# Shift and scale worked out in four quarters of the channels, with the first three weight slabs taken quarter by quarter, in a one-core transformer layer

## The chip, the cores and the metric

One core of one Trainium2 chip runs the whole program. The metric is the device time of one execution in microseconds. Three runs of the kernel before took 1442.45, 1448.24 and 1449.41 us, so the median is 1448.24 us. One more execution was profiled, and all rows below come from it.

## The reference, cut to what matters

```python
def modulation(cv, w, b):
    m = jax.nn.silu(cv) @ w + b                      # w is 1024 x 6144
    return [a[:, None, :] for a in jnp.split(m, N_MOD, axis=-1)]
...
m_lat = modulation(c, w_mod[l], b_mod[l])
m_ctx = modulation(c_ctx[None], w_mod[l], b_mod[l])
u_lat = rmsnorm(x, g[0]) * (1.0 + m_lat[1]) + m_lat[0]
u_ctx = rmsnorm(ctx, g[0]) * (1.0 + m_ctx[1]) + m_ctx[0]
y_lat, y_ctx = token_mixer(u_lat, u_ctx, ...)         # starts with u @ w_in, 1024 x 8704
x = x + m_lat[2] * rmsnorm(y_lat, g[1])
f_lat = moe(...)                                      # 32 experts, 1024 x 2048 and 1024 x 1024 each
x = x + m_lat[5] * rmsnorm(f_lat, g[3])
```

There are 256 latent and 256 context tokens of 1024 channels, in float32. Only the first two of the six modulation vectors, shift and scale, matter to the change. They are needed before the first product with w_in.

## The kernel before, in words

**Set-up (lines 104 to 148).** Two rows of c and c_ctx go through a sigmoid and are transposed to `csT`, which is 128 channels by 8 groups of channels by 32 columns (two of them used). The tokens x and ctx are loaded into `xt` and `xn[:, 2:4]` by two transfers of 1 MB, which SP issues (lines 120 and 121).

**Shift and scale (`mod_first`, line 168, and `mod_columns`, line 154).** For each half `hv` of the channels, 4 MB of w_mod are loaded in eight transfers of 512 KB into the tiles tagged `oh` and `oa`. 32 matmuls, each with 32 columns of the array and 256 moving columns, gather the sums in the PSUM tile `pm`. ScalarE copies `pm` out to `mr`, TensorE transposes it to `pmt`, and VectorE adds the bias into `mod`.

**Inputs (lines 278 to 287).** ScalarE squares each of four token tiles and takes a root, VectorE scales the tile, TensorE transposes it in blocks into `xT`, and ScalarE copies these to `xnT`, which has one column block for each of eight groups of 128 channels.

**Modulated inputs (`modulated`, line 293).** For each channel group `k`, two ScalarE activations of 256 tokens apply scale and shift in `xnT`. VectorE rounds the result to `uh` (fp32r) and puts the rest in `ul`.

**Slabs.** A slab is 1024 rows by 256 columns of w_in, which is 1 MB in runs of 1 KB (`slab`, line 225). A ScalarE cast gives its upper part `hi`, a VectorE subtraction the rest `lo`; `hl` holds both, in two buffers. Each product is three matmuls (`mm3`, line 246). The first three slabs, two of the forget gates (`pf`, 512 moving columns) and one of the values (`pv`, 256 moving columns), are worked through in two halves of the channels (lines 315 to 329). The third slab is loaded over `xn`, and so its transfer waits for the last transpose of the inputs.

**What sets the order.** A scheduler orders each engine's instructions when the program is built; each engine then runs its list in that order, and SP issues its transfers in its order too. After the slabs above come more slabs and the recurrence (up to some 300 us), attention, merge and router (to some 515 us), and the experts. The experts' weights come through a ring of ten 2 MB buffers (`Ring`, line 897), which is refilled as TensorE finishes with a buffer.

Of the kernel before, what the change touches and what calls it, by code (L numbers as in the profile page):

```python
# [11 lines left out]
F32 = mybir.dt.float32  # L12
F32R = mybir.dt.float32r
# [9 lines left out]
P = 128  # L23
D = 1024
KT = 8
# [14 lines left out]
def hybrid_layer(ctx, tc, x, c, ctx_in, c_ctx, w_mod, b_mod, norm_g, w_in, hgrn_lb, hgrn_norm_g,  # L40
                 qk_norm_g, w_branch, w_out, router_w, router_b, w_up, b_up, w_down, b_down,
                 rope_c, rope_s, out):
    nc = tc.nc
    pe, act, dve, pool = nc.tensor, nc.scalar, nc.vector, nc.gpsimd
# [46 lines left out]
    def mmps(name):  # L91
        return ps.tile([P, 512], F32, tag="mm", bufs=4, name=name)
# [24 lines left out]
    nc.scalar.dma_start(small_l, hgrn_lb.rearrange("d l (k p) -> (d l k) p", p=P))  # L117
    xn = xp.tile([P, 4, D], F32, tag="xn", name="xn")
    xnT = xp.tile([P, KT, 512], F32, name="xnT")
    nc.sync.dma_start(xt, x.rearrange("b (t p) d -> p (b t) d", p=P))  # L120
    nc.sync.dma_start(xn[:, 2:4], ctx_in.rearrange("b (t p) d -> p (b t) d", p=P))

# [44 lines left out]

    def mod_first(hv):

        pm = trps(f"pm0{hv}")  # L170
        wv = w_mod[0, :, 0:2048].rearrange("(q k p) (i f) -> p q k i f", k=2, p=P, i=2)
        for q in range(4):
            if q % 2 == 0:
                wq = lp.tile([P, 2, 2, 2, 512], F32, tag=("oh", "oa")[q // 2], name=f"wm0{hv}{q}")
            wr = wq[:, q % 2]
            for k in range(2):
                nc.sync.dma_start(wr[:, k], wv[:, q, k, :, hv * 512:(hv + 1) * 512])
                for j in range(4):
                    pe.matmul(pm[32 * j:32 * j + 32, 0:256], csT[:, 2 * q + k],
                              wr[:, k, j // 2, (j % 2) * 256:(j % 2) * 256 + 256],  # L180
                              start=q + k == 0, stop=q + k == 4)
        mod_columns(pm, 256, 2, (8, 2), 4 * hv, f"0{hv}")

    def mod_steps(ch, acc):

# [51 lines left out]

    def split(hi, lo, src):

        act.copy(hi, src)  # L240
        dve.tensor_sub(lo, src, hi)  # L241
# [4 lines left out]
    def mm3(o, a, b, k, opens, closes):  # L246

        i = pe.matmul(o, a[0], b[0], start=k == 0 and opens, stop=False)  # L248
        if k == 0 and not opens:
            tc.keep_in_program_order(i)  # L250
        pe.matmul(o, a[0], b[1], start=False, stop=False)  # L251
        pe.matmul(o, a[1], b[0], start=False, stop=k == KT - 1 and closes)  # L252

    def chan_major(sl, mh, ml, n, outs, hfs=(0, 1)):

        for hf in hfs:
            hi, lo = sl(hf)
            for cc in range(2):
                for kk in range(4):
                    k = hf * 4 + kk  # L260
                    wh, wl = hi[:, kk, cc * P:(cc + 1) * P], lo[:, kk, cc * P:(cc + 1) * P]
                    mm3(outs[cc], (wh, wl), (mh[hf][:, kk, 0:n], ml[hf][:, kk, 0:n]), k,
                        cc == 0 or n == 512, cc == 1 or n == 512)

    def tok_major(sl, mh, ml, tts, outs, hfs=(0, 1), closes=False):

        for hf in hfs:
            hi, lo = sl(hf)
            for i, tt in enumerate(tts):
                for kk in range(4):  # L270
                    k = hf * 4 + kk
                    th, tl = mh[hf][:, kk, tt * P:(tt + 1) * P], ml[hf][:, kk, tt * P:(tt + 1) * P]
                    mm3(outs[i], (th, tl), (hi[:, kk], lo[:, kk]), k, i % 2 == 0, i % 2 == 1 or closes)
# [16 lines left out]
    uh, ul = [[t[:, hv] for hv in range(2)] for t in uhl]  # L290
    wi = w_in[0]

    def modulated(hv):
        ks_ = slice(4 * hv, 4 * hv + 4)
        for r in range(2):
            dve.scalar_tensor_tensor(aff0[:, r, ks_], mod[:, r, 8 + 4 * hv:12 + 4 * hv], 1.0, gT[:, ks_],
                                     op0=ALU.add, op1=ALU.mult)
        for k in range(4 * hv, 4 * hv + 4):
            for r in range(2):
                sl = xnT[:, k, r * 256:(r + 1) * 256]  # L300
                act.activation(sl, sl, AF.Identity, bias=mod[:, r, k:k + 1], scale=aff0[:, r, k:k + 1])
            dve.tensor_copy(uh[hv][:, k % 4], xnT[:, k])
            dve.tensor_sub(ul[hv][:, k % 4], xnT[:, k], uh[hv][:, k % 4])

    def part(sl, hf):

        hl = sl(hf)
        return lambda h: hl if h == hf else sl(h)

    def both(sl):  # L310

        hl = [sl(hf) for hf in range(2)]
        return lambda h: hl[h]

    mod_first(0)
    firsts = [(part(slab(wi[:, 2048 + 1024 * d:2304 + 1024 * d], f"f{d}0"), 0),
               [mmps(f"pf0{d}{cc}") for cc in range(2)]) for d in range(2)]
    modulated(0)
    sl_i = slab(wi[:, 1024:1280], "i0", xp.tile([P, 4, D], F32, tag="xn", name="wi0").rearrange("p a b -> p (a b)")[:, 0:2048])
    mod_first(1)  # L320
    for sl, pf in firsts:
        chan_major(sl, uh, ul, 512, pf, (0,))
    pv0 = [hgps(f"pv0{i}") for i in range(2)]
    pvs0 = [pv0[i // 2][:, (i % 2) * 256:(i % 2) * 256 + 256] for i in range(4)]
    tok_major(sl_i, uh, ul, range(4), pvs0, (0,))
    modulated(1)
    for sl, pf in firsts:
        chan_major(sl, uh, ul, 512, pf, (1,))
    tok_major(sl_i, uh, ul, range(4), pvs0, (1,))

    nc.sync.dma_start(hg, hgrn_norm_g.rearrange("l p -> p l"))
    nc.sync.dma_start(rw.rearrange("p (j i) e -> p j i e", i=2), router_w.rearrange("l (j p i) e -> p (l j) i e", p=P, i=2))
# [910 lines left out]
```

## Time and profile before

| | us |
|---|---|
| median of 3 runs | 1448.24 |
| lowest, highest run | 1442.45, 1449.41 |
| profiled execution, its own time | 1452.08 |
| its span | 1450.2 |
| TensorE matmuls busy | 1339.9 (92%) |
| VectorE busy | 504.5 (35%) |
| ScalarE busy | 354.5 (24%) |
| DMA read from HBM | 479.15 MB, 331 GB/s over the span |

The profiled execution lies 3.84 us above the median, and its time is 1.9 us longer than its span. Busy shares are means over stages with different limits, so they say little about one stage. TensorE can run at one of two clock levels, 1.2 and 2.4 GHz, and the profile gives the granted clock of a stretch as a share of the upper one. A timeline row gives start, duration, engine, line, operation, tiles, shape and count, and in brackets how long the engine stood idle before and what ended that.

### The profile page before, as it was taken

The page shows a single profiled execution, that of the slowest core. Times are in us where ns is not written, and L with a number is a line of the kernel's source. Part 1 is how long each engine was busy: PE and PEld are TensorE (multiplying, and loading weights), DVE is VectorE, ACT ScalarE, POOL GpSimd, SP SyncE. Part 2 cuts the span into 40 slices and gives each one's busy share as a digit, 9 for nine tenths or more (in the row PEclk, how much of TensorE's full clock was granted, in tenths as well). Part 3 has the DMA queues.
Part 4 walks back from the last instruction along what each step waited for, and adds up shares of the span by engine and source line. Part 5 has one row for each costly group of instructions (what it writes and reads, how often), then busy time and mean ns, then how long its engine had stood idle before and what let it go on. Part 6 is the DMA issues. An engine that isn't in the chain of part 4 may idle for free. (4 is left out here: it accounts for less than half of the span.)

```text
span 1450.2 us, 18975 instructions
## 1 busy us (share of the span) xinstructions
PE 1339.9 (92%) x8151; PEld 743.0 (51%) x8151; DVE 504.5 (35%) x917; ACT 354.5 (24%) x648; POOL 3.8 (0%) x16
## 2 busy tenths in 40 slices
PE   6999999998999989999998897998899889889887
PEld 3789788898889943333432342342243233224222
DVE  4697777678875341111101011120011010111012
ACT  5444444456555330110100010010010010001002
POOL 0000000000000000000000000000000000000000
PEclk9999999999999899999999999999999999999999
DMA  9535342246649499999999999999999999999994
GB/s 343 173 120 168 121 147 90 88 128 228 225 153 344 150 388 428 428 427 428 426 428 428 428 427 425 427 428 428 427 428 428 427 426 427 428 428 427 428 425 161
DMA packets 88529, 481.52 MB, mean 332 GB/s; under 512 B 5604, under 2 KB 56264, under 8 KB 62072
## 3 DMA queue, kind: packets, MB, share of 16 engines
q1 hardware_dynamic: 87536, 479.24, 81.5%
q8 instruction: 66, 1.08, 0.3%
q10 hardware_dynamic: 776, 0.84, 0.2%
q14 instruction: 23, 0.19, 0.0%
q0 software_dynamic: 128, 0.16, 0.0%
HBM read 479.15 MB, written 1.08 MB: 331 GB/s over the span
## 5 line engine op out<-in xcount | busy, mean ns | idle before, releaser
L847 PE MATMUL pu<-w,xe 128*64 128x512 f32 x2048 | 457.9, 597 | 61.1 <-DMA w<-in_w_up_dram 61.1
L847 PEld LDWEIGHTS pu<-w,xe 128*64 128x64 f32 x2048 | 142.6, 137 | 360.0 <-issue 249.6
L991 DVE TENSOR_SCALAR gl<-pu 128x512 f32<-128x512 f32 (+1 forms) x33 | 22.2, 675 | 617.8 <-PE pu L847 602.5
L847 PE MATMUL py<-w,aT 128*64 128x512 f32 (+1 forms) x1040 | 227.3, 589 | 1.9 <-ACT aT L1033 1.9
L847 PEld LDWEIGHTS py<-w,aT 128*64 128x64 f32 x1040 | 70.9, 137 | 153.5 <-issue 119.3
L992 ACT ACTIVATE sg<-gl 128x512 f32<-128x512 f32 (+1 forms) x33 | 20.2, 616 | 514.9 <-PE pat L850 479.8
L1046 ACT COPY ysb<-py 128x512 f32<-128x512 f32 x31 | 18.1, 585 | 242.2 <-PE py L847 242.2
L847 PE MATMUL acc<-ysb,cw 64*128 64x512 f32 (+2 forms) x260 | 65.8, 608 | 2.7 <-DVE ysb L1189 1.9
L847 PE MATMUL pgx<-oh,xt 128*128 128x256 f32 x256 | 60.2, 394 | 0.0
L847 PEld LDWEIGHTS pgx<-oh,xt 128*128 128x128 f32 x256 | 46.7, 199 | 16.8 <-issue 5.7
L248 PE MATMUL pf<-uh,hlf 128*128 128x512 f32 x128 | 52.3, 414 | 3.1 <-ACT hlf L240 3.1
L252 PE MATMUL pf<-uh,hlf 128*128 128x512 f32 x128 | 52.9, 415 | 0.0
L251 PE MATMUL pf<-ul,hlf 128*128 128x512 f32 x128 | 52.4, 411 | 0.0
L975 DVE TENSOR_SCALAR xe<-pgx,aff,mod 128x256 f32<-128x256 f32 x32 | 17.4, 543 | 88.9 <-PE pgx L847 88.9
L983 DVE TENSOR_SCALAR ow<-iota,posb,comb 128x128 f32<-128x128 f32 x64 | 19.2, 343 | 57.4 <-PE pcw L850 29.5
L248 PE MATMUL pga<-uh,hlga 128*128 128x256 f32 x128 | 36.9, 288 | 2.4 <-ACT hlga L240 2.4
L252 PE MATMUL pga<-uh,hlga 128*128 128x256 f32 x128 | 36.3, 284 | 1.0 <-DVE hlga L241 1.0
L248 PE MATMUL pv<-hli,uh 128*128 128x256 f32 x128 | 36.5, 285 | 0.0
L847 PEld LDWEIGHTS acc<-ysb,cw 64*128 64x128 f32 (+1 forms) x260 | 23.4, 186 | 25.6 <-issue 21.9
L251 PE MATMUL pv<-hli,uh 128*128 128x256 f32 x128 | 36.3, 284 | 0.0
L251 PE MATMUL pga<-ul,hlga 128*128 128x256 f32 x128 | 36.2, 283 | 0.0
L252 PE MATMUL pv<-hli,ul 128*128 128x256 f32 x128 | 36.2, 283 | 0.0
(382 smaller groups left out, 2069.8 us busy)
## 6 DMA issues: line engine op xcount, KB each, us to landing
w<-in_w_up_dram SPq DMA_DIRECT2D x128, 2048.0 KB, 39.1
w<-in_w_down_dram SPq DMA_DIRECT2D x62, 2048.0 KB, 39.1
wm<-in_w_mod_dram SPq DMA_DIRECT2D x16, 1024.0 KB, 4.8
wm<-in_w_mod_dram SPq DMA_DIRECT2D x16, 512.0 KB, 10.3
wf<-in_w_in_dram SPq DMA_DIRECT2D x8, 1024.0 KB, 5.2
wga<-in_w_in_dram SPq DMA_DIRECT2D x8, 1024.0 KB, 5.1
wwb<-in_w_branch_dram SPq DMA_DIRECT2D x8, 1024.0 KB, 6.3
wi<-in_w_in_dram SPq DMA_DIRECT2D x4, 1024.0 KB
```

The costliest lines, as they stand in the source:

```text
L248: i = pe.matmul(o, a[0], b[0], start=k == 0 and opens, stop=False)
L251: pe.matmul(o, a[0], b[1], start=False, stop=False)
L252: pe.matmul(o, a[1], b[0], start=False, stop=k == KT - 1 and closes)
L847: tc.keep_in_program_order(pe.matmul(*args, **kw))
L975: dve.tensor_scalar(xe[:, k], pg, aff2[:, k:k + 1], mod[:, 0, 24 + k:25 + k], op0=ALU.mult, op1=ALU.add)
L983: dve.tensor_scalar(ow[:, tt], view(iota, [[0, 2], [1, CAP]]), posb[:, tt, e:e + 1], comb[:, tt, e:e + 1], op0=ALU.is_equal, op1=ALU.mult)
L991: dve.tensor_scalar(gl, glu_ps, 7.0, None, op0=ALU.min)
L992: act.activation(sg, gl, AF.Sigmoid, scale=1.702)
L1046: act.copy(ysb, py)
```

## The change

Each of the two halves of shift and scale becomes two quarters of 256 channels. A quarter's weights are two transfers of 1 MB in runs of 1 KB (runs of 2 KB before), one for shift and one for scale, into a whole `oh` or `oa` tile (`mod_load`). The first quarter is issued ahead of x and ctx. `mod_first` works with 128 moving columns instead of 256, so it has 32 matmuls for a quarter where it had 32 for a half. The first three slabs are loaded in halves (`send`), and are split and multiplied in quarters of the channels, one after the other for all three slabs. What is computed stays the same.

```diff
+    wmq = [lp.tile([P, 2, KT, 256], F32, tag=t, name="wm0" + t) for t in ("oh", "oa")]
+
+    def mod_load(q):
+
+        wv = w_mod[0, :, 0:2048].rearrange("(k p) (i f) -> p k i f", p=P, i=2)
+        for i in range(2):
+            nc.sync.dma_start(wmq[q % 2][:, i], wv[:, i, :, q * 256:(q + 1) * 256])
+
+    mod_load(0)
     nc.sync.dma_start(xt, x.rearrange("b (t p) d -> p (b t) d", p=P))
     nc.sync.dma_start(xn[:, 2:4], ctx_in.rearrange("b (t p) d -> p (b t) d", p=P))
...
-    def mod_first(hv):
-
-        pm = trps(f"pm0{hv}")
-        wv = w_mod[0, :, 0:2048].rearrange("(q k p) (i f) -> p q k i f", k=2, p=P, i=2)
-        for q in range(4):
...
-                nc.sync.dma_start(wr[:, k], wv[:, q, k, :, hv * 512:(hv + 1) * 512])
-                for j in range(4):
-                    pe.matmul(pm[32 * j:32 * j + 32, 0:256], csT[:, 2 * q + k],
...
-        mod_columns(pm, 256, 2, (8, 2), 4 * hv, f"0{hv}")
+    def mod_first(q):
+
+        pm, wq = trps(f"pm0{q}"), wmq[q % 2]
+        for k in range(KT):
+            for j in range(4):
+                pe.matmul(pm[32 * j:32 * j + 32, 0:P], csT[:, k], wq[:, j // 2, k, j % 2 * P:(j % 2 + 1) * P],
+                          start=k == 0, stop=k == KT - 1)
+        mod_columns(pm, P, 2, (8, 1), 2 * q, f"0{q}")
...
-    def modulated(hv):
-        ks_ = slice(4 * hv, 4 * hv + 4)
+    def modulated(q):
+        hv, ks_ = q // 2, slice(2 * q, 2 * q + 2)
...
-    mod_first(0)
-    firsts = [(part(slab(wi[:, 2048 + 1024 * d:2304 + 1024 * d], f"f{d}0"), 0),
...
+    send(0, 0)
+    send(1, 0)
+    mod_load(1)
+    send(2, 0)
+    for q in range(4):
+        mod_first(q)
+        modulated(q)
+        if q < 2:
+            mod_load(q + 2)
+        if q == 0:
+            for n in range(3):
+                send(n, 1)
+        hv = q // 2
+        for n in range(3):
+            hl = ip.tile([P, 2, 2, 256], F32R, tag="hl", bufs=2, name=f"hl0{q}{n}")
+            hi, lo = hl[:, 0], hl[:, 1]
+            split(hi, lo, wr0[n][:, 2 * q:2 * q + 2])
+            for cc in range(2 if n < 2 else 4):
+                for kk in range(2):
...
```

SP's list, from its third transfer on, before and then in the changed kernel (`wm` is w_mod, `wf` and `wi` the slabs, `xt` and `xn` the inputs):

```order
L120 DMA xt<-in_x_dram 128x2x1024
L121 DMA xn<-in_ctx_dram 128x2x1024
L177 DMA wm_214<-in_w_mod_dram 128x2x512 x4
L177 DMA wm_235<-in_w_mod_dram 128x2x512 x4
L228 DMA wf_263<-in_w_in_dram 128x8x256
L228 DMA wf_270<-in_w_in_dram 128x8x256
L228 DMA wi_295<-in_w_in_dram 128x8x256
L177 DMA wm_298<-in_w_mod_dram 128x2x512 x4
```

```order
L126 DMA wm0oh<-in_w_mod_dram 128x8x256 x2
L129 DMA xt<-in_x_dram 128x2x1024
L130 DMA xn<-in_ctx_dram 128x2x1024
L318 DMA wf_217<-in_w_in_dram 128x4x256
L318 DMA wf_218<-in_w_in_dram 128x4x256
L126 DMA wm0oa<-in_w_mod_dram 128x8x256 x2
L126 DMA wm0oh<-in_w_mod_dram 128x8x256
L318 DMA wi_219<-in_w_in_dram 128x4x256
L126 DMA wm0oh<-in_w_mod_dram 128x8x256
L318 DMA wf_217<-in_w_in_dram 128x4x256
L318 DMA wf_218<-in_w_in_dram 128x4x256
L318 DMA wi_219<-in_w_in_dram 128x4x256
```

Two transfers of w_mod now stand ahead of the inputs, and the transfer of the third slab, which is laid over `xn`, stands ahead of half of the third quarter of w_mod and of the slabs' second halves.

ScalarE's list at the inputs, before and then in the changed kernel (`mr` is the copy of the sums for shift and scale):

```order
L280 ACTIVATE xnT,ssq<-xt 128x1024 x2
L221 ACT_TABLE_LOAD
L221 ACTIVATE rs_146<-ssq,epsc 128x1 x2
L280 ACTIVATE xnT,ssq<-xn 128x1024 x2
L221 ACTIVATE rs_146<-ssq,epsc 128x1 x2
```

```order
L167 COPY mr_264<-pm_231 128x128
L282 ACTIVATE xnT,ssq<-xt 128x1024 x2
L223 ACT_TABLE_LOAD
L223 ACTIVATE rs_150<-ssq,epsc 128x1 x2
L282 ACTIVATE xnT,ssq<-xn 128x1024 x2
L223 ACTIVATE rs_150<-ssq,epsc 128x1 x2
L242 CAST hl_285<-wf_217 128x512
```

The copy of the first quarter's sums now stands ahead of the squares of x.

TensorE's list at the border of the third and the fourth quarter in the changed kernel, and VectorE's list at the same place (`hl_605` and `hl_620` are the fourth quarter's weights; `bf` and `bu` belong to the experts' bias):

```order
L254 MATMUL pv_225<-hl_529,ul 128x256
L171 MATMUL pmt_591<-ident,mr_589 128x128
L250 MATMUL pf_220<-uh,hl_605 128x512
L250 MATMUL pf_221<-uh,hl_605 128x512
L250 MATMUL pf_222<-uh,hl_620 128x512
```

```order
L174 TENSOR_TENSOR mod<-pmt_591,bT 128x2x2 x2
L298 SCALAR_TENSOR_TENSOR aff_78<-mod,gT 128x2
L548 CAST bu_87<-bf_1488 32x512
L298 SCALAR_TENSOR_TENSOR aff_78<-mod,gT 128x2
L243 TENSOR_TENSOR hl_620<-wf_218,hl_620 128x512
L550 TENSOR_TENSOR bf_1488<-bf_1488,bu_87 32x512
L548 CAST bu_87<-bf_1488 32x512
L304 CAST uh<-xnT 128x512
```

Between the transpose `pmt_591` and the first product of the fourth quarter TensorE has nothing else in its list; in the kernel before, the transpose of the second half stood among the products `pv` of the first half.

ScalarE's list where the first stage ends, before and then in the changed kernel (`hlq` is the weight of the next slab):

```order
L548 ACTIVATE sg_646<-pf_275 128x512
L548 ACTIVATE sg_650<-pf_276 128x512
L553 COPY fl_0_636<-fl_0_636 128x512
L240 CAST hlq_661<-wq_658 128x1024
L564 COPY vt_655<-pv_395 128x512
```

```order
L584 COPY vt_746<-pv_224 128x512
L568 ACTIVATE sg_737<-pf_222 128x512
L573 COPY fl_0_727<-fl_0_727 128x512
L568 ACTIVATE sg_741<-pf_223 128x512
L584 COPY vt_746<-pv_225 128x512
L242 CAST hlq_752<-wq_749 128x1024
```

The cast for the next slab stood ahead of both copies of `pv` and now stands behind them, and one of these copies stands ahead of two of the sigmoids.

## Rows read from the trace of the kernel before

**Rows 1.** The chain that ended last, by engine and line (first entries on one row).
```profile
DMA w<-in_w_up_dram 24%; DMA w<-in_w_down_dram 11%; PE pu L847 1%; PE py L847 1%; PE acc L847 1%; DVE og L1200 0%; PE rbpb L209 0%; DVE ysb L1189 0%; ACT jk L1193 0%; PE pcw L850 0%; ACT g3t L215 0%; DVE g3t L207 0%; ACT ysb L1046 0%; DVE gl L991 0%; DVE og L1194 0%
```

**Rows 2.** Stretches: length, PE busy (count), PE clock, DMA share, GB/s.
```profile
100.00:150.00 50.00, 49.81 (x423) 1.00 0.40 129
...
600.00:700.00 100.00, 100.00 (x474) 1.00 1.01 427
```

**Rows 3.** Waits of the DMA queue on SP, 420 to 560 us: total, times, longest.
```profile
SPq L925 <- PE pu L847: 31.4, 6, 16.2
```

**Rows 4.** Timeline of SP's transfers, first inputs and third slab.
```profile
1.72 0.41 SPq L120 DMA_DIRECT2D xt<-in_x_dram  x1
2.73 0.39 SPq L121 DMA_DIRECT2D xn<-in_ctx_dram  x1
...
22.54 0.37 SPq L228 DMA_DIRECT2D wi<-in_w_in_dram  x1
```

**Rows 5.** Stretches of one us, columns as in rows 2: x, w_mod, slab.
```profile
5.00:6.00 1.00, 0.46 (x3) 1.00 1.01 414
13.00:14.00 1.00, 1.00 (x10) 1.00 1.05 389
24.00:25.00 1.00, 0.44 (x2) 1.00 1.10 350
```

**Rows 6.** Timeline of ScalarE, inputs to the first modulated channels.
```profile
6.80 1.06 ACT L280 ACTIVATE xnT<-xt 128x1024 f32<-128x1024 f32 x1 [1.95 <-DMA xt<-in_x_dram]
...
20.96 1.07 ACT L287 COPY xnT<-xT 128x512 f32<-128x512 f32 x2 [0.52 <-PE xT L286]
...
24.00 0.37 ACT L158 COPY mr<-pm 128x256 f32<-128x256 f32 x1 [0.86 <-PE pm L179]
25.35 1.58 ACT L301 ACTIVATE xnT<-xnT,mod,aff 128x256 f32<-128x256 f32 x3 [0.99 <-DVE aff L296]
```

**Rows 7.** Timeline of VectorE, the scaling of the last token tile.
```profile
14.18 0.75 DVE L282 TENSOR_SCALAR xn<-xn,rs 128x1024 f32<-128x1024 f32 x1
```

**Rows 8.** Timeline of TensorE, start and end of the first stage.
```profile
11.64 0.69 PE L286 MATMUL xT<-ident,xn 128*128 128x128 f32 x2 [3.48 <-DVE xn L282]
12.25 1.08 PE L179 MATMUL pm<-wm,csT 128*32 128x256 f32 x8
...
22.44 1.50 PE L179 MATMUL pm<-wm,csT 128*32 128x256 f32 x22
...
27.92 0.79 PE L248 MATMUL pf<-uh,hlf 128*128 128x512 f32 x1 [3.06 <-ACT hlf L240]
...
64.33 0.39 PE L248 MATMUL pf<-uh,hlf 128*128 128x512 f32 x1
64.56 0.39 PE L251 MATMUL pf<-ul,hlf 128*128 128x512 f32 x1
...
70.65 0.28 PE L252 MATMUL pv<-hli,ul 128*128 128x256 f32 x1
...
70.89 0.28 PE L251 MATMUL pq<-ul,hlq 128*128 128x256 f32 x1
72.31 0.39 PE L252 MATMUL pq<-uh,hlq 128*128 128x256 f32 x1 [1.14 <-DVE hlq L241]
```

**Rows 9.** Stretches at the lower clock level, columns as in rows 2.
```profile
28.00:33.00 5.00, 5.00 (x12) 0.50 1.06 380
...
341.00:344.00 3.00, 3.00 (x16) 0.50 1.05 394
474.00:484.00 10.00, 10.00 (x49) 0.50 0.56 229
```

**Rows 10.** Timeline of TensorE, the wait ahead of the second such stretch.
```profile
340.44 0.39 PE L248 MATMUL pga<-uh,hlga 128*128 128x256 f32 x1 [2.23 <-ACT hlga L240]
```

**Rows 11.** VectorE by line, 50 to 75 us: busy, mean ns.
```profile
L530 DVE TENSOR_TENSOR bf<-bf,bu 32x512 f32<-32x512 f32 x4 | 2.7, 678 | 0.1
L241 DVE TENSOR_TENSOR hlq<-wq,hlq 128x1024 fp32r<-128x1024 f32 x2 | 2.4, 1210 | 0.0
```

More of the change, by code (lines that the diff above doesn't have):

```diff
@@ L119, in hybrid_layer @@
     xnT = xp.tile([P, KT, 512], F32, name="xnT")
+    wmq = [lp.tile([P, 2, KT, 256], F32, tag=t, name="wm0" + t) for t in ("oh", "oa")]
+    def mod_load(q):
+        wv = w_mod[0, :, 0:2048].rearrange("(k p) (i f) -> p i k f", p=P, i=2)
+        for i in range(2):
+            nc.sync.dma_start(wmq[q % 2][:, i], wv[:, i, :, q * 256:(q + 1) * 256])
+    mod_load(0)
     nc.sync.dma_start(xt, x.rearrange("b (t p) d -> p (b t) d", p=P))
@@ L166, in mod_columns @@
                               view(bT, md, start), op=ALU.add)
-    def mod_first(hv):
-        pm = trps(f"pm0{hv}")
-        wv = w_mod[0, :, 0:2048].rearrange("(q k p) (i f) -> p q k i f", k=2, p=P, i=2)
-        for q in range(4):
[L173 to L176, printed above, removed]
-                nc.sync.dma_start(wr[:, k], wv[:, q, k, :, hv * 512:(hv + 1) * 512])
-                for j in range(4):
-                    pe.matmul(pm[32 * j:32 * j + 32, 0:256], csT[:, 2 * q + k],
-                              wr[:, k, j // 2, (j % 2) * 256:(j % 2) * 256 + 256],
-                              start=q + k == 0, stop=q + k == 4)
-        mod_columns(pm, 256, 2, (8, 2), 4 * hv, f"0{hv}")
+    def mod_first(q):
[5 more added lines that the diff above has]
+        mod_columns(pm, P, 2, (8, 1), 2 * q, f"0{q}")
     def mod_steps(ch, acc):
@@ L252, in mm3, with chan_major @@
         pe.matmul(o, a[1], b[0], start=False, stop=k == KT - 1 and closes)
-    def chan_major(sl, mh, ml, n, outs, hfs=(0, 1)):
-        for hf in hfs:
+    def chan_major(sl, mh, ml, n, outs):
+        for hf in range(2):
             hi, lo = sl(hf)
@@ L263, in chan_major, with tok_major @@
                         cc == 0 or n == 512, cc == 1 or n == 512)
-    def tok_major(sl, mh, ml, tts, outs, hfs=(0, 1), closes=False):
-        for hf in hfs:
+    def tok_major(sl, mh, ml, tts, outs, closes=False):
+        for hf in range(2):
             hi, lo = sl(hf)
@@ L291, in hybrid_layer @@
     wi = w_in[0]
-    def modulated(hv):
-        ks_ = slice(4 * hv, 4 * hv + 4)
+    def modulated(q):
+        hv, ks_ = q // 2, slice(2 * q, 2 * q + 2)
         for r in range(2):
-            dve.scalar_tensor_tensor(aff0[:, r, ks_], mod[:, r, 8 + 4 * hv:12 + 4 * hv], 1.0, gT[:, ks_],
+            dve.scalar_tensor_tensor(aff0[:, r, ks_], mod[:, r, 8 + 2 * q:10 + 2 * q], 1.0, gT[:, ks_],
                                      op0=ALU.add, op1=ALU.mult)
-        for k in range(4 * hv, 4 * hv + 4):
+        for k in range(2 * q, 2 * q + 2):
             for r in range(2):
@@ L303, in modulated @@
             dve.tensor_sub(ul[hv][:, k % 4], xnT[:, k], uh[hv][:, k % 4])
-    def part(sl, hf):
-        hl = sl(hf)
-        return lambda h: hl if h == hf else sl(h)
     def both(sl):
@@ L313, in both @@
         return lambda h: hl[h]
-    mod_first(0)
-    firsts = [(part(slab(wi[:, 2048 + 1024 * d:2304 + 1024 * d], f"f{d}0"), 0),
[L317 to L322, printed above, removed]
-    pv0 = [hgps(f"pv0{i}") for i in range(2)]
-    pvs0 = [pv0[i // 2][:, (i % 2) * 256:(i % 2) * 256 + 256] for i in range(4)]
@@ L325, in hybrid_layer, with send @@
[L325 to L329, printed above, removed]
+    wr0 = [raw_tile("wf00"), raw_tile("wf10"), xp.tile([P, 4, D], F32, tag="xn", name="wi0").rearrange("p a b -> p (a b)")[:, 0:2048]]
+    wr0 = [w.rearrange("p (k f) -> p k f", k=KT) for w in wr0]
+    def send(n, hf):
+        c0 = (2048, 3072, 1024)[n]
+        nc.sync.dma_start(wr0[n][:, 4 * hf:4 * hf + 4], wi[hf * 512:(hf + 1) * 512, c0:c0 + 256].rearrange("(k p) f -> p k f", p=P))
@@ new lines, in hybrid_layer @@
+    firsts = [(None, [mmps(f"pf0{d}{cc}") for cc in range(2)]) for d in range(2)]
+    pv0 = [hgps(f"pv0{i}") for i in range(2)]
+    send(0, 0)
[17 more added lines that the diff above has]
+                for kk in range(2):
+                    k = 2 * q + kk
+                    mh, ml = uh[hv][:, k % 4], ul[hv][:, k % 4]
+                    if n < 2:
+                        cs = slice(cc * P, (cc + 1) * P)
+                        mm3(firsts[n][1][cc], (hi[:, kk, cs], lo[:, kk, cs]), (mh, ml), k, True, True)
+                    else:
+                        ts_ = slice(cc * P, (cc + 1) * P)
+                        mm3(pv0[cc // 2][:, cc % 2 * 256:cc % 2 * 256 + 256], (mh[:, ts_], ml[:, ts_]), (hi[:, kk], lo[:, kk]), k,
+                            cc % 2 == 0, cc % 2 == 1)
```

## The prediction

> **What bounds the kernel now.** I read the chain of waits first. Nearly all of it is transfers of expert weights [rows 1], and from the experts on these run without a gap at 427 GB/s [rows 2]. That stretch cannot be shortened, only begun earlier or later. So I read next what starts it: the queue on SP waited 31.4 us in all between 420 and 560 us for TensorE to free the buffers of the ring [rows 3]. Before that TensorE is the bound: from 100 to 150 us it is busy 49.81 us of 50 [rows 2]. A microsecond won or lost on TensorE in the first stage therefore moves the experts, and with them the end, by about a microsecond. Then I read the first stage on the timeline. SP issues x at 1.72 us, ScalarE squares it from 6.80, the last token tile is scaled by 14.93, the last transposes free `xn` at 22.54, the sums for shift and scale of the first half are copied at 24.00, the first slab product runs at 27.92 after a wait of 3.06, and the last one of the third slab ends at 70.77 [rows 4, 6, 7, 8]. The reader should see that this stage was late because of shift and scale, not because of the inputs, and that TensorE had work from 27.92 on.
>
> **The inputs move back.** Two transfers (2.10 MB) now stand ahead of x. They come in runs of 1 KB, and slabs with such runs moved at 350 GB/s [rows 5], so x waits 6.0 us more and could be squared at 12.8 instead of 6.80 [rows 6]. The row beside it shows 389 GB/s with runs of 2 KB, so the size of a run does count here. The Trainium skill ("DMA: Bandwidth & Descriptors", Specifications) has line rate from runs of 512 bytes on; by that the quarter would move at 389 GB/s and the whole sum would be 0.6 us smaller. The two rows speak against it.
>
> But ScalarE's list has the copy of the quarter's sums ahead of the squares. x's own 1.05 MB took 2.5 us at 414 GB/s [rows 5], so the stream began at about 4.3, and the quarter is in at 10.3. Its 32 matmuls stand twice each in the trace. At the start TensorE runs them slowly: 8 entries of 256 columns took 1.08 us [rows 8], so 64 of 128 columns take some 4.2 us, and the copy ends near 14.7. Inputs then trail by 7.9 us instead of 6.0. The scaling of the last tile moves from 14.93 to 22.8, and to some 23.2 with a split that VectorE now does ahead of it.
>
> The transposes follow. ScalarE's eight copies (0.53 us each) now alternate with activations (0.53 each) [rows 6]; the last transposes wait for six copies and three activations, 4.8 us, and end at 28.5 if TensorE is at its upper clock. At the rate of the first two (0.61 us for two [rows 8]) they would end near 31. I take 29.5. Steady products thus begin at **29.5**, between 28.5 and 31, against 27.92 now. What the early first quarter wins in shift and scale is gone before it is used.
>
> SP's third slab waits for these transposes too, and 5 MB are queued behind it. It is issued near 29.3 instead of 22.54, and the last of the 5 MB (3.0 us each) lands near 47. The fourth quarter needs it after 50, so this costs nothing; if the products began four microseconds earlier, it would be late next.
>
> **The work from there to the end of the third slab.** There are 96 products of 512 and 96 of 256 columns as before, at 0.23 and 0.12 us [rows 8]: 33.6 us. Sums: 22 entries of 256 columns took 1.50 us [rows 8], so an entry of 128 costs 0.034; about 186 of 256 entries fall here: 6.3 us, where 64 entries of 0.068, 4.4 us, fell in the stage before. A mod chain (copy, transpose, add, two activations, rounding) lasts 1.35 us from copy to activation [rows 6] and 1.5 more, 2.9 in all. In the second quarter 58 entries of sums (2.0 us) run beside it, and 0.9 is left; in the third, 64 entries, and 0.7 is left. In the fourth nothing runs beside it. There the copy is done early, but VectorE has three pieces of the experts' bias between scale and rounding (the longest 0.68 us [rows 11], by which I estimate 1.5 for the three), which adds 1.1 beyond the activations, and the lower part comes 0.4 late: 4.0. The second channel group of the first quarter is 0.8 late. Waits: 6.4. The sum is 29.5 + 33.6 + 6.3 + 6.4 = 75.8 us against 70.77, 5.0 more. Counted alike, the kernel before gives 27.92 + 33.6 + 4.4 and 2.8 for its stretch at the lower clock, 68.7, so the count is 2.1 short for switches between kinds of matmul. The new list has fewer of these; I add 0.5: **+5.5**.
>
> **The next slab.** Its cast stands behind both copies of `pv`. Before, its lower part came 1.5 us after the end of `pv` (72.31 against 70.77 [rows 8]). Now it takes a copy (0.59), a cast (1.05) and a subtraction of 1.21 [rows 11] after that end, 2.8, and two sigmoids that wait behind the first copy push some 1.7 of VectorE's work ahead of it: 4.5 at most. The loss is 1.3 to 3.0; I take **+2.4**, near the upper end, since each of these stands on a list that is worked in order.
>
> **The clock.** A wait of 3.06 us was followed by 5 us at a granted clock of 0.50, which is the lower level of 1.2 GHz, one of 2.23 by at least 3 [rows 8, 9, 10]. Half of such a stretch is lost, 1.5 to 2.8 us. The new waits are of 4.0 and 4.5; the second is broken by two products, and my lengths are estimates, so I count one stretch: **+2.2**, between 0 and 5.
>
> In all +10.1 us. The profiled execution would go from 1452.08 to 1462.2. It lies 3.84 above the median of 1448.24, so the median should be about **1458**. Costed at nothing: the splits in quarters (as many elements, twice as many instructions, beside TensorE's products as long as these last) and SP's 16 transfers in place of 21 (one stream, busy up to 27 us).
>
> **Rivals.**
>
> *The waits are covered (0.27).* Shorter chains than I read, an upper clock at the transposes, and no new stretch at the lower one: start 28.5, waits of 3, that is 71.4, and 1.3 for the next slab. +1.9, so 1450; 1448 to 1454. For it: the scheduler put sums beside two of the four chains. Against: in-order lists on three engines.
>
> *Every burst falls cold (0.15).* Both new waits bring the lower level: +12.3, 1460, and 1463 if the transposes also end at 31. For it stand both waits of the trace. The Trainium skill ("TensorE: Matmul & The Clock Gate", HAM oscillation) describes this for loops of short bursts with waits between, where each burst starts cold; by it, this is the case to expect of work cut into quarters. The trace agrees for a wait of 2.23 us.
>
> *Faster: the inputs are not held back (0.20).* If the engines mixed the transfers, x would land near 9.5, the transposes would end at 24.5 and products run from 23.5. With 2 us of waits that is 23.5 + 33.6 + 6.3 + 2.0 = 65.4, or -5.4: 1443. It needs the squares of x to start before 10 us, and TensorE's waits to stay under 3. Against it: ctx, as large as x, was issued 1.0 us behind it [rows 4]; evenly mixed, both would have landed after 5 us of data, yet x was squared 5.1 us after its issue, so transfers went in their order [rows 5, 6]. For it: the order of lists is no time, and 2.9 of the old wait plus the stretch at the lower clock (2.8) are there to win.
>
> That the change is not made is excluded: the lists show the first quarter ahead of x and four rounds of products.
>
> **How the numbers follow.** The forecast (1455 to 1461) has 0.38. The range runs from 1446, which leaves out most of the faster case, to 1464, which holds the cold one. A difference of 0.5% (7.2 us, about what runs that spread from 1442 to 1449 can tell) puts the limits at 1441.0 and 1455.5. Half of the faster case lies below, 0.09, since a stretch at the lower clock such as the one from 474 to 484 us, with TensorE busy throughout [rows 9], may come or not come, worth 5 us. Slower takes 0.32 of the forecast and all of the cold case, 0.47; the rest, 0.44, is no change.
>
> **What would show it.** Right: squares of x near 14.7, the last transposes near 29, the third slab issued right after them, a wait of TensorE of some 4 us after the transpose of the fourth quarter, `pv` ending near 76 to 78, and all later stages shifted by one amount up to the experts. Wrong: squares before 10 us, or `pv` done before 71. If `pv` ends as I say and the end does not move, the link from TensorE to the ring is what failed.

## The result, and the profile after

| | kernel before | changed kernel |
|---|---|---|
| median of 4 runs, us | 1445.71 | 1463.16 |
| lowest, highest run | 1442.45, 1449.41 | 1459.77, 1464.02 |
| profiled execution, its span | 1452.08, 1450.2 | 1464.02, 1462.4 |

The changed kernel takes 1.0104 times as long (95% interval 1.008 to 1.0128), so it is slower by 12 to 19 us. Another series of runs gave 1463.01 against 1445.79, a ratio of 1.0109 (1.0081 to 1.0137). The forecast was 1458, in a range up to 1464.

The rows below answer to those shown of before. First the timeline of SP's transfers, which is to be compared with [rows 4].

```profile
1.71 1.25 SPq L126 DMA_DIRECT2D wm0oh<-in_w_mod_dram  x2
3.00 1.20 SPq L129 DMA_DIRECT2D xt<-in_x_dram  x1
...
30.60 0.37 SPq L318 DMA_DIRECT2D wi<-in_w_in_dram  x1
```

Next the timeline of ScalarE, from the inputs to the next slab's cast (compare [rows 6]).

```profile
14.57 0.27 ACT L167 COPY mr<-pm 128x128 f32<-128x128 f32 x1 [4.12 <-PE pm L182]
14.74 1.06 ACT L282 ACTIVATE xnT<-xt 128x1024 f32<-128x1024 f32 x1
...
73.80 0.62 ACT L242 CAST hl<-wi 128x512 fp32r<-128x512 f32 x1 [5.96 <-PE pf L254]
74.33 2.01 ACT L192 ACTIVATE macc<-wm,csT 128x2048 f32<-128x2048 f32 x1
76.35 1.28 ACT L568 ACT_TABLE_LOAD   x1
77.65 1.09 ACT L568 ACTIVATE sg<-pf 128x512 f32<-128x512 f32 x2
...
81.07 2.01 ACT L242 CAST hlq<-wq 128x1024 fp32r<-128x1024 f32 x2
```

x is squared at 14.74 instead of 6.80, right behind the copy of the first quarter's sums. Behind the third slab's cast stand one piece of the later modulation vectors (`macc`, 2.01 us) and a table load of 1.28. Only then come the sigmoids, and the next slab's cast behind these.

The timeline of VectorE at the fourth quarter shows the experts' bias pieces (`bu`, `bf`) between the scale (`aff`) and the rounding (`uh`).

```profile
65.92 0.14 DVE L298 SCALAR_TENSOR_TENSOR aff<-mod,gT 128x2 f32<-128x2 f32 x1
65.99 0.67 DVE L243 TENSOR_TENSOR hl<-wf,hl 128x512 fp32r<-128x512 f32 x1
66.59 0.67 DVE L550 TENSOR_TENSOR bf<-bf,bu 32x512 f32<-32x512 f32 x1
67.30 0.42 DVE L548 CAST bu<-bf 32x512 bf16<-32x512 f32 x1
67.74 0.43 DVE L304 CAST uh<-xnT 128x512 fp32r<-128x512 f32 x1
```

The timeline of TensorE holds what these lists cost it (compare [rows 8]; `pq` are the products of the next slab).

```profile
28.94 0.47 PE L250 MATMUL pf<-uh,hl 128*128 128x512 f32 x1
29.43 1.14 PE L288 MATMUL xT<-ident,xn 128*128 128x128 f32 x8
30.33 0.47 PE L253 MATMUL pf<-ul,hl 128*128 128x512 f32 x1
...
68.22 1.19 PE L250 MATMUL pf<-uh,hl 128*128 128x512 f32 x4 [2.96 <-DVE uh L304]
...
78.59 0.28 PE L254 MATMUL pv<-hl,ul 128*128 128x256 f32 x1
82.19 0.39 PE L250 MATMUL pq<-uh,hlq 128*128 128x256 f32 x1 [3.32 <-ACT hlq L242]
...
85.06 0.58 PE L254 MATMUL pq<-uh,hlq 128*128 128x256 f32 x1 [2.38 <-DVE hlq L243]
```

Products run without transposes between them from 30.33, the third slab ends at 78.87 instead of 70.93, and the next slab's first lower part comes at 85.06 instead of 72.31.

The stretches show the clock behind each of the two waits. A row here has more columns than [rows 2, 9]: length, busy time and count of PE, PEld, DVE, ACT and POOL, then PE clock, DMA share and GB/s.

```profile
6.00:10.00 4.00, 1.17 (x7) 0.59 (x7) 1.00 (x12) 0.12 (x1) 0.00 (x0) 1.00 1.10 352
...
18.00:28.00 10.00, 6.26 (x22) 3.24 (x23) 4.58 (x10) 7.08 (x17) 0.00 (x0) 0.52 0.97 310
...
70.00:72.00 2.00, 2.00 (x6) 1.52 (x6) 1.93 (x4) 0.00 (x0) 0.00 (x0) 0.50 0.48 201
84.00:89.00 5.00, 3.94 (x18) 3.94 (x19) 5.00 (x6) 0.75 (x1) 0.00 (x0) 0.50 0.32 98
...
354.00:357.00 3.00, 2.99 (x25) 2.81 (x26) 1.90 (x5) 2.70 (x5) 0.00 (x0) 1.00 1.08 399
486.00:496.00 10.00, 10.00 (x49) 10.00 (x49) 1.61 (x3) 1.77 (x3) 0.00 (x0) 0.50 0.55 225
600.00:700.00 100.00, 100.00 (x474) 38.16 (x472) 15.96 (x30) 11.02 (x22) 0.00 (x0) 1.00 1.01 427
```

The first row is for the start, below. Both waits are followed by the lower level (0.50), where the forecast counted one. A third stretch at that level begins near 18 us, within a wait of 4.35 us that ends at 19.57, and lies over the transposes of the inputs. The work that stood at 0.50 from 341 us before [rows 9] runs from 354 us here, at 1.00. The one of 10 us in the attention's end is in both profiles, 12 us later in this one. And the experts' transfers run at 427 GB/s as before.

The waits of SP's queue from 432 to 572 us show that the link to the experts held. They are those of [rows 3] to the tenth.

```profile
SPq L945 <- PE pu L867: 31.4, 6, 16.2
```

So nearly all that was lost was lost in the first stage and at the next slab: the slab after that one, the gate slab, ends 13.1 us later (98.96 against 85.89). The last product of the attention's keys ends 14.0 us later (303.47 against 289.43). 2.0 us come back in the attention, where a wait of 1.68 us stands in the place of the 2.23 of [rows 10] and no lower level follows it. SP issues the experts' first transfer 12.0 us later (436.89 against 424.93), and the span is 12.2 longer.

### The profile page after: what moved, and what is told of

Read it like the earlier page. It is cut to its first block, busy times and chain, and to the rows that moved or that the text cites. A ratio compares the mean times of both kernels' runs of the same rounds, so it can differ in the third digit from the quotient of the medians.

```text
span 1462.4 us, 19259 instructions
## 1 busy us (share of the span) xinstructions
PE 1342.9 (92%) x8279; PEld 751.0 (51%) x8279; DVE 508.0 (35%) x931; ACT 355.3 (24%) x656; POOL 3.8 (0%) x16
## 5 line engine op out<-in xcount | busy, mean ns | idle before, releaser
L254 PE MATMUL pf<-uh,hlf 128*128 128x512 f32 x96 | 39.3, 409 | 0.0
L1003 DVE TENSOR_SCALAR ow<-iota,posb,comb 128x128 f32<-128x128 f32 x64 | 19.2, 344 | 57.6 <-PE pcw L870 29.5
L250 PE MATMUL pf<-uh,hlf 128*128 128x512 f32 x96 | 38.9, 406 | 0.0
L253 PE MATMUL pf<-ul,hlf 128*128 128x512 f32 x96 | 38.9, 406 | 0.0
L194 DVE SCALAR_TENSOR_TENSOR macc<-wm,csT,macc 128x2048 f32<-128x2048 f32 x14 | 32.8, 2346 | 9.3 <-DMA wm<-in_w_mod_dram 9.3
L870 PEld LDWEIGHTS pat<-ident,gl 128*128 128x128 f32 x128 | 17.8, 208 | 25.8 <-issue 24.3
L867 PE MATMUL pu<-bu,sel 96*64 96x512 bf16 x128 | 20.7, 399 | 7.8 <-PEq L1110 5.4
```

Source lines behind the costliest of these rows:

```text
L194: dve.scalar_tensor_tensor(acc, wr, csT[:, k, 0:1], acc, op0=ALU.mult, op1=ALU.add)
L867: tc.keep_in_program_order(pe.matmul(*args, **kw))
L870: tc.keep_in_program_order(pe.transpose(*args))
L1003: dve.tensor_scalar(ow[:, tt], view(iota, [[0, 2], [1, CAP]]), posb[:, tt, e:e + 1], comb[:, tt, e:e + 1], op0=ALU.is_equal, op1=ALU.mult)
```

## The experiments

All timed ratios are to the kernel before. For each kernel the table has three ends on TensorE's timeline, in us: of the third slab (`pv`), of the first gate slab (`pg`) and of the attention's keys (`pk`). Behind the keys the profiles differ mainly by stretches at the lower clock, so the third end is the finest measure of the first stages. Two profiles of the same changed kernel (the rows changed and a1_again) differ by 0.6, 1.1 and 1.1 us at the three ends, and a gain below that tells nothing.

| kernel | third slab | gate slab | keys | ratio (95% interval) |
|---|---|---|---|---|
| before | 70.93 | 85.89 | 289.43 | |
| changed | 78.87 | 98.96 | 303.47 | 1.0104 (1.008 to 1.0128) |
| a1_again | 78.29 | 97.87 | 302.35 | 1.0109 (1.0081 to 1.0137) |
| e1_inputs_first | 77.17 | 95.00 | 298.93 | 1.0078 (1.0052 to 1.0103) |
| e3_cast_early | 79.01 | 93.15 | 297.68 | 1.0063 (1.0038 to 1.0088) |
| e2_pipelined | 70.53 | 85.28 | 290.63 | 1.0011 (0.9994 to 1.0027) |
| e7_bias_late | 77.86 | 98.57 | 305.44 | 1.0111 (1.0088 to 1.0135) |
| e4_warm | 78.91 | 99.36 | 304.13 | 1.0125 (1.0097 to 1.0154) |
| e4b_warm_short | 77.49 | 96.32 | 301.84 | 1.0105 (1.0079 to 1.013) |
| e5_all | 69.56 | 84.09 | 287.67 | 0.9999 (0.9983 to 1.0015) |
| e8_sums_amid | 67.05 | 81.03 | 286.42 | 0.9996 (0.9975 to 1.0016) |
| e6_before_cast | 70.22 | 83.98 | 289.44 | 1.0008 (0.9992 to 1.0024) |

In the two kernels with added products the third slab's end is taken as the start of these.

**The changed kernel once more (a1_again).** No edit.

> The changed kernel once more, unaltered, so that the experiments have it beside them and the size of the loss gets a second measurement. By the first stage of its trace (12 us later than before from the first slabs to the end) it should lie 10 to 14 us above the kernel before. If the first comparison's 17 us holds again, some 4 us come from outside the shift that the trace shows, such as a stretch at the lower clock in a later stage that one kernel has more often than the other; then the stages behind the first should show it.

The loss of some 17 us between medians held. At the keys it was 12.9 us, against 14.0 in the first profile, so some of the 17 lies outside the first stages. Its profile has the stretch at the lower clock near the attention's end too, as the row shows:

```profile
484.00:494.00 10.00, 10.00 (x50) 10.00 (x50) 1.61 (x3) 2.21 (x3) 0.00 (x0) 0.51 0.59 239
```

In the five profiles that have it (before, the changed kernel twice, e3, e4b), 1023.3 to 1026.7 us lie between SP's first transfer of w_up (424.93 before, 436.89 after) and the span's end, and 1019.4 to 1022.3 in those that have it not. Only a profile shows the stretch itself; of the other runs there are times and mean clocks. Beside this series seven runs of the kernel before took 1443.0 to 1446.6 us at a mean clock of 0.990 to 0.993, and four 1449.3 to 1452.0 at 0.986 to 0.989. Of the eight runs of the changed kernel in two series, seven took 1462.6 to 1464.0 at 0.982 to 0.986, and one 1459.77 at 0.989. So it seems that the median of before is here one mostly without such a stretch, and that of the changed kernel one mostly with it; this is read from times and clocks and is not shown. In a later series, that of e2, the kernel before was slower more often: 12 of its 23 runs took 1448.5 to 1452.4 us. Why the stretch comes or stays away was not tried.

**Inputs first (e1_inputs_first).**

```diff
-    mod_load(0)
     nc.sync.dma_start(xt, ...)
     nc.sync.dma_start(xn[:, 2:4], ...)
+    mod_load(0)
```

> The first quarter's two transfers of shift and scale stand behind x and ctx instead of ahead of them; all else is the changed kernel. If the inputs held back are a cost of the change: x is squared near 6.8 us again, the last input is scaled near 15 instead of 22.5, the first steady products run near 25 instead of 29.8, and everything later comes about 4 to 5 us earlier, 1458 to 1459. The rival: the start is set by shift and scale anyway, and what is won at the inputs is lost in a wait for the first quarter's sums or for a later quarter, whose transfers now come later; then the start of the products moves by less than 1.5 us and the time stays at 1461 to 1464.

The timeline of TensorE shows the start, the fourth quarter and the next slab,

```profile
23.11 1.51 PE L182 MATMUL pm<-wm0oh,csT 128*32 128x128 f32 x46
25.02 0.33 PE L171 MATMUL pmt<-ident,mr 128*128 128x128 f32 x1 [0.40 <-ACT mr L167]
...
27.44 0.73 PE L250 MATMUL pf<-uh,hl 128*128 128x512 f32 x2 [1.75 <-DVE uh L304]
...
66.96 1.15 PE L250 MATMUL pf<-uh,hl 128*128 128x512 f32 x2 [4.03 <-DVE uh L304]
...
77.35 0.39 PE L250 MATMUL pq<-uh,hlq 128*128 128x256 f32 x1 [0.18 <-ACT sg L568]
```

and ScalarE's the next slab's cast, which the scheduler moved in this kernel as well:

```profile
74.34 1.05 ACT L242 CAST hlq<-wq 128x1024 fp32r<-128x1024 f32 x1 [1.64 <-PE pf L254]
75.40 1.28 ACT L568 ACT_TABLE_LOAD   x1
```

The inputs held back are a cost at the start: products begin at 27.44 instead of 30.33. They did not begin at 25, as expected, since the sums now stand behind the transposes and their chain runs bare (1.51 of sums and 2.8 to the first product). Much of the gain was lost in the fourth quarter's wait, 4.03 here, so that 1.1 to 1.7 us are left at the end of the third slab. The keys end 3.4 to 4.5 us earlier and the median is 1457.1 against 1463.0, but this is not the price of the inputs alone: the cast now stands ahead of the table load, and the next slab begins 0.18 us behind the third instead of 3.32. The next experiment shows what that move alone is worth.

**The next slab's cast early (e3_cast_early).**

```diff
+        if pr_ == 0:
+            hq = both(slab(wi[:, c0:c0 + 256], "q0"))
...
-        sl = slab(wi[:, c0:c0 + 256], f"q{pr_}")
+        sl = hq if pr_ == 0 else slab(wi[:, c0:c0 + 256], f"q{pr_}")
```

> The next slab is split ahead of the four sigmoids and the other work behind the third slab, instead of behind them; all else is the changed kernel. If ScalarE's list is what makes TensorE wait for 6.3 us behind the third slab: the two waits at that slab (3.32 and 2.38 us) shrink to 2 us or less together, the stretch at the granted clock of 0.50 behind them goes, and all that follows comes 4 to 7 us earlier, 1456 to 1459. The rival: the sigmoids are wanted as urgently, and the wait moves to the next product that needs them or to the lower parts on VectorE; then the slab begins earlier but the next stage (the gate slab, last seen ending at 92.8) ends no more than 1 us earlier, and the time stays at 1461 to 1464.

The timeline of ScalarE has the cast ahead of the table load and the sigmoids:

```profile
76.36 1.03 ACT L242 CAST hlq<-wq 128x1024 fp32r<-128x1024 f32 x1
77.41 1.28 ACT L570 ACT_TABLE_LOAD   x1
78.70 0.60 ACT L570 ACTIVATE sg<-pf 128x512 f32<-128x512 f32 x1
```

and TensorE's has the next slab 0.3 us behind the third:

```profile
79.35 0.39 PE L250 MATMUL pq<-uh,hlq 128*128 128x256 f32 x1 [0.34 <-ACT sg L570]
```

Waits of 3.32 and 2.38 shrank to one of 0.34, the clock stayed at 1.00 behind it, and the gate slab's wait of 1.19 at 86.80 gave back only a part. The third slab ends where it did (79.01), the keys 4.7 to 5.8 us earlier, and the median is 1457.55. The place of the split in the lists of ScalarE (the cast) and VectorE (the subtraction) made those waits, and not its transfer, which SP issued at 48.73 us here and at 48.89 in the changed kernel.

**Chains a quarter ahead (e2_pipelined).**

```diff
-        mod_first(q)
-        modulated(q)
+        if q == 0:
+            mod_first(0)
+            modulated(0)
...
+        if q < 3:
+            mod_first(q + 1)
+            modulated(q + 1)
```

> The sums, columns and activations of the next quarter are issued ahead of this quarter's slab products instead of behind them, so that each chain can run beside products; all else is the changed kernel. If the chains standing bare between two quarters are a cost of the change: the wait of 2.96 us ahead of the fourth quarter falls under 0.5 us, no stretch at the lower clock follows it, the third slab ends near 74 instead of 78.5, and all later stages come 4 to 6 us earlier, more if the next slab's cast also comes earlier: 1455 to 1458. The rival: the sums of a quarter now stand in TensorE's list ahead of products and wait for their transfers, so that as much is lost in new waits between 30 and 60 us as is won behind them; then the third slab still ends after 77 and the time stays at 1461 to 1464.

TensorE's timeline has the third quarter's sums and the third slab's end:

```profile
40.70 1.96 PE L182 MATMUL pm<-wm0oh,csT 128*32 128x128 f32 x64
43.16 0.27 PE L171 MATMUL pmt<-ident,mr 128*128 128x128 f32 x1
...
70.25 0.28 PE L254 MATMUL pv<-hl,ul 128*128 128x256 f32 x1
...
72.25 0.39 PE L254 MATMUL pq<-uh,hlq 128*128 128x256 f32 x1 [1.48 <-DVE hlq L243]
```

and ScalarE's the cast that moved with it, now ahead of `macc`:

```profile
67.99 1.04 ACT L242 CAST hlq<-wq 128x1024 fp32r<-128x1024 f32 x1
...
73.48 2.02 ACT L192 ACTIVATE macc<-wm,csT 128x2048 f32<-128x2048 f32 x1
```

No wait over 0.4 us is left between the transposes and the third slab's end, which comes 8.3 us earlier. Of the waits at the next slab the first went and one of 1.48 is left, since the scheduler then put the cast behind the second sigmoid; before, one of 1.14 stood there [rows 8]. The keys end 1.2 us behind those of before, and the median ratio is 1.0011. This one edit takes back nearly all of the loss, with the inputs still held back. It does two things at once, the chains and the cast; e3 tells them apart, since there the third slab's end stayed.

**The bias pieces late (e7_bias_late).**

```diff
-        bf_ = lp.tile([P, 512], F32, tag="lt", bufs=2, name=f"bf{q}")[0:NE]
+        bf_ = hp_.tile([P, 512], F32, tag="sg", bufs=2, name=f"bf{q}")[0:NE]
```

> The pieces of the experts' bias take buffers that come free only behind the sigmoids, so VectorE has none of them between the fourth quarter's scale and its rounding; all else is the changed kernel. If these pieces lengthen the fourth quarter's wait by 1.1 us, as predicted: the wait of 2.96 us falls to about 1.9, the rounding follows the second activation at once, and later stages come about 1 us earlier, or 2 to 3 if the shorter wait is no longer followed by the lower clock. The rival: ScalarE's activations alone set the wait; then it stays within 0.4 us of 2.96.

TensorE's timeline shows the shorter wait, and two that came later:

```profile
67.73 1.22 PE L250 MATMUL pf<-uh,hl 128*128 128x512 f32 x2 [2.06 <-DVE uh L304]
...
149.64 0.38 PE L254 MATMUL pq<-uh,hlq 128*128 128x256 f32 x1 [1.21 <-DVE hlq L243]
...
210.41 0.39 PE L254 MATMUL pq<-uh,hlq 128*128 128x256 f32 x1 [1.52 <-DVE hlq L243]
```

The pieces did cost 0.9 of the 1.1 predicted. But taken from there they stood in VectorE's way in later slabs, and the keys ended 2 to 3 us later. The wait of 2.06 was still followed by the lower clock.

**The waits filled (e4_warm, e4b_warm_short).** Before `modulated(3)` and before the next slab stand unused products, 6 and 10 in the first of the two kernels, 3 and 6 in the second.

```diff
+            for _ in range(6):
+                tc.keep_in_program_order(pe.matmul(wt3, ident, xt[:, 0, 0:512], start=True, stop=True))
```

> Products whose result nobody reads (6 and 10, each 512 columns) stand in the two long waits of TensorE, the one of the fourth quarter and the one behind the third slab; the waits themselves are not removed. If the lower clock behind the waits is a cost of its own: the granted clock stays near 1.00 from 69 to 73 us and from 83 to 90 us, and later stages come 2.5 to 4 us earlier, 1459 to 1461. The rival: the clock falls in the same places, or does not matter because the engines that feed TensorE set the pace there; then the stages move by less than 1 us, or come later by as much as the extra products push the needed ones, up to 2 us.

TensorE's timeline has the six of the first version (two entries stand for each):

```profile
65.30 5.31 PE L331 MATMUL warm<-xt,ident 128*128 128x512 f32 x12
...
87.09 0.68 PE L250 MATMUL pq<-uh,hlq 128*128 128x256 f32 x1
```

One such product took 0.88 us, so the fill reached past both waits and pushed the next slab to 87.09, and this run does not tell what the lower clock cost. So it was made shorter:

> Products whose result nobody reads again, now 3 and 6: six took 5.3 us in the longer version, about 0.85 each, so they should fill some 2.6 of the fourth quarter's wait and 5.1 of the one behind the third slab without pushing the needed products. If the lower clock is a cost of its own: the granted clock stays near 1.00 behind both waits, the third slab ends about 1.3 us earlier than in the changed kernel, the gate slab 2.5 to 3.5 us earlier, 1459 to 1461. The rival: the gate slab ends within 1 us of the changed kernel's (97.9 to 99.0), and the lower clock cost nothing that the engines ahead of TensorE did not set anyway.

The same stretches as in the changed kernel, now at the upper level:

```profile
70.00:72.00 2.00, 2.00 (x9) 1.45 (x10) 1.90 (x5) 0.00 (x0) 0.00 (x0) 1.00 0.50 209
84.00:89.00 5.00, 5.00 (x42) 5.00 (x43) 5.00 (x6) 1.44 (x2) 0.00 (x0) 1.00 0.59 193
```

The clock follows what TensorE did in the wait, and filling it is worth 1.6 to 2.6 us at the gate slab. Only 0.5 to 1.6 of that is left at the keys, and nothing in the medians (1.0105). Later stages of this profile had three short stretches at the lower clock, between 353 and 405 us, which the changed kernel's had not, so the clock's share of the final time stays open.

**Combinations (e5_all, e8_sums_amid) and the cast in the kernel before (e6_before_cast).** e5 joins the edits of e1, e2 and e3. e8 adds to it that the first quarter's sums and activations are issued amid the transposes:

```diff
         act.copy(xnT[:, k], pt)
+        if k == 2:
+            mod_first(0)
+        if k == 4:
+            modulated(0)
```

> Three edits of the changed kernel at once: x and ctx ahead of the first quarter's transfers, each quarter's chain ahead of the quarter's products before it, and the next slab split ahead of the sigmoids. If the loss of the change is these three in sum: 3 to 4 us from the start, 4 from the fourth quarter, 4 to 5 from the next slab, in all 11 to 13, so the time is that of the kernel before within 4 us, 1443 to 1450. The rival: they overlap (what is won early waits later for the fourth quarter's transfers or for ScalarE's list), and the time stays above 1452.

> The three edits together, and the first quarter's sums now stand amid the transposes, behind the third of eight groups, with their activations behind the fifth. In the three edits together the first steady product ran at 26.07 us, 4.3 behind the last transposes (46 entries of sums 1.5, then the chain of copy, transpose and activations). If that bare chain is the last part of the start that costs: products begin near 23.5, the third slab ends 2 to 2.5 us earlier than in the three edits together (whose gate slab ended at 84.1), the last attention product of the keys ends near 285.5 instead of 287.7, and the time is 1443 to 1446, some 0.2% under the kernel before. The rival: ScalarE's copies and activations are the bound there and the sums only push the transposes back; then products begin after 25.5 and nothing is won.

> The kernel before, with nothing but the next slab's split issued ahead of the sigmoids. In the kernel before TensorE waited 1.14 us for that slab's lower part. If the split's place in the lists costs in either kernel what its wait shows: the wait goes and the time is 1 to 1.5 us less than before, inside what can be told apart, where the same edit gave the changed kernel 4.6 to 5.7 us at the end of the first head pair. The rival: the early split pushes ScalarE's sigmoids and VectorE's scan back in the kernel before, and the next wait (for the decay's pieces, behind the gate slab) grows by as much or more: 0 to 3 us slower.

The timeline of TensorE in e8:

```profile
17.86 2.47 PE L182 MATMUL pm<-wm0oh,csT 128*32 128x128 f32 x60
...
23.26 0.73 PE L250 MATMUL pf<-uh,hl 128*128 128x512 f32 x2 [0.79 <-DVE uh L298]
```

The three edits bring the changed kernel to the time of before (0.9999), 1.8 us ahead of it at the keys. With the sums amid the transposes products begin at 23.26, the third slab ends 3.9 us ahead of before, the keys 3.0, and the ratio is 0.9996 (0.9975 to 1.0016). Some of that lead is clock: e8 has no stretch at 0.50 before the keys, and the kernel before has one from 28 to 33 us [rows 9], for which the forecast counted 2.8 us. At the keys e8 is 16 to 17 us better than the change as made, but against the kernel before 3 us can't be told from nothing in the times. In e6 the gate slab came 1.9 us earlier (0.7 of it already at the third slab, ahead of the edit's place) and the keys not at all: a wait of 0.97 for VectorE's part of the second pair's slab (at 135.37) is new in it. Part of e8's lead was lost on the same way (4.9 at the gate slab, 3.0 at the keys), with 0.98 at the same product. Whether the quarters themselves win anything over halves that are issued just as early was not tried.

## Why the prediction was right, step by step

**Sign and mechanisms held, the size with luck.** The median of 1463.16 lies outside the forecast's own 1455 to 1461 and 0.84 us under the end of the range, which had been drawn to hold the cold case. What came is nearer to that rival (0.15) than to the forecast (0.38): both new waits brought the lower level, and the transposes ended late. By its own terms the rival's upper figure is 1462 (12.3 and 1.5 above 1448.24), not 1463; that it hits the median is chance, since 3 us of this come from the base, below.

TensorE's delay reaches the experts with 12.0 of the 14.0 us at the keys, and SP's wait of 31.4 us is unchanged. The inputs were held back: squares at 14.74 (forecast 14.7), last transposes done at 30.57 (29.5, between 28.5 and 31), the third slab issued at 30.60 (29.3) at no cost. The forecast had put the transposes between TensorE's two rates; they came out near the slow one, with the stretch at 0.50 over them, TensorE busy throughout from 25 us on. The price of the order itself is small: 1.1 to 1.7 us at the third slab's end in e1, and 1.0 between e2 and e5 (70.53 and 69.56), where the cast's place, the other difference, does not move that end in e3.

**The first quarter's runs of 1 KB.** From 6 to 10 us transfers moved at 352 GB/s in the stretches of after (the forecast used 350); the same weights in runs of 2 KB had moved at 389 [rows 5]. The Trainium skill ("DMA: Bandwidth & Descriptors", Specifications) has line rate from 512 bytes on; the measurement decides against it again.

**The step up to the end of the third slab was mis-sized in two terms that nearly cancel.** It was to end 5.5 us later without the clock, at 76.3; it ended at 78.87, of which some 1.4 is the stretch at the lower clock behind the fourth quarter's wait. That is some 1.2 more than forecast: 0.6 from the start, 2.1 from switches, less 1.6 of waits. The waits sum to 4.84 (0.36, 0.17, 0.53, 0.57, 2.96 and 0.25), where 6.4 was forecast. But the step "The new list has fewer of these; I add 0.5", said of switches between kinds of matmul, failed. From the first products (about 30.1) to 78.87 are 48.8 us; less 33.6 of products, 6.3 of sums, 4.84 of waits and 1.4 of clock, 2.6 remain for switches, where the forecast added 0.5; by the same count the kernel before had 2.1.

**The next slab's term was half of what it cost.** The copy, cast and subtraction with the sigmoids between, +2.4, became +4.8: 6.2 us from the end of `pv` to the first lower part (85.06 less 78.87) against 1.4. The forecast had counted the work behind the copies of `pv`. It had not counted what stands ahead of the sigmoids on ScalarE's list, `macc` with 2.01 us and the table load with 1.28: from `macc` at 74.33 to the end of the cast at 83.08 ScalarE had no idle time, so in that order the cast could not come sooner. e3, which moves the cast ahead of the table load and the sigmoids, took back 4.7 to 5.8 with the clock behind it.

**The clock.** Behind the new waits two stretches came, not one, and a third lay at the start, inside the term for the transposes. The rival that every burst falls cold had this right where the forecast had not. The lower level followed the waits of 2.96, of 3.32 with 2.38, and in e7 of 2.06. The Trainium skill ("TensorE: Matmul & The Clock Gate", HAM oscillation) describes such bursts, each cold behind its wait. The trace agrees, though most of these waits are shorter than those of the Trainium skill's example. The price, as half of the time at 0.50, is some 1.4 and 2.2 us, 3.6 in all against 2.2, inside its bounds of 0 to 5. In e4b, where the waits were filled, only 0.5 to 1.6 us of it were left at the keys.

**What the forecast could have had.** 7.9 us at the third slab, 4.8 at the next and 2.2 of clock behind it make 14.9, of which 13.1 are left at the end of the gate slab; on the way the kernel before had two waits of 0.38 that the changed kernel has not. The span is 12.2 longer, against 10.1 forecast. So the profiled execution was forecast at 1462.2 and took 1464.02, 1.8 more. The other 3 us between 1458 and 1463.16 are the base: the profiled execution of before lay 3.84 above its median of three runs, the one after only 0.86 above its own. With the fourth run the median of before fell to 1445.71, so that its profile lay 6.37 above. Of the 17.45 us between the medians 11.94 lie between the two profiled executions, and 5.51 are this difference in base. That the base differs because the stretch of 10 us near the attention's end [rows 9] is in most runs of the changed kernel and in fewer of the kernel before is likely from their times and clocks, and not shown.

## What to carry to other kernels

Work cut into finer pieces must have each piece's preparation issued a piece ahead; here issue order alone was worth 12 to 13 us at the keys (e2). It only took back the loss: no kernel here is clear of noise faster than the one before. Read the in-order list of the engine that prepares the next operand right through, with what stands ahead of the instruction that you think it waits for. After an edit read these lists again at other places too: in e1 the scheduler moved a cast that the edit did not name, and much of the gain came behind it. And look at which rare stretches the one profiled execution contains before its offset from the median is carried over to the changed kernel.

## What the runs showed of the hardware that was not expected

- TensorE's clock fell to 0.50 for some 10 us in a stretch with the engine busy throughout, in the profiles of before, the changed kernel (twice), e3 and e4b, and not in those of e1, e2, e4, e5, e6, e7 and e8. From the experts' first transfer to the end of the span it takes 1025.3 us in the mean with it and 1020.7 without. One profile cannot tell whether a kernel has it.
- A wait of TensorE of 2.06 us was followed by the lower level (e7), and with 2.7 us of unused products in the wait of 2.96 the clock stayed at the upper one (e4b). Waits of near length went both ways: one of 1.75 us was followed by the lower level (e2, ending at 341.07 us), one of 1.84 was not (e6, at 340.25).
- At the start the granted clock does not tell TensorE's pace. From 18 to 28 us TensorE did the same work in the changed kernel, at 0.52 in the mean (22 entries, 6.26 us busy, in the row after the change), and in e7, where the column reads 1.00:

```profile
18.00:28.00 10.00, 6.27 (x22) 3.25 (x23) 4.58 (x10) 7.08 (x17) 0.00 (x0) 1.00 1.00 319
```

- A product of float32 with 512 moving columns took 0.88 us (e4, granted clock 1.00) where the fp32r products of that size took 0.23 [rows 8], nearly four times as long.
